# Gathering the base inverse's diagonal blocks once, and another order of the second group of pieces, in a hybrid encoder layer

## The chip, the cores and the metric

The kernel runs on one core of a Trainium2 chip. The metric is the device time of one execution in microseconds (us); lower is better. Engines are named as in the profile: PE (matrix products), PEld (its weight loads), DVE (vector), ACT (scalar and activation functions), POOL (GpSimd) and SP, whose queue issues all the DMAs of this kernel.

## What is computed

One layer of a bidirectional encoder trunk on x of 1024 tokens by 1024 features, float32:

```python
proj = rms_norm(x) @ w_in                       # columns split into aq, ak, av, dqkv, dgate, dalpha, dbeta
attn_o = window_attention(rope(aq), rope(ak), av, sink)        # 8 heads, 2 kv heads, +-128 tokens
dn_o = gated_deltanet(dqkv, dgate, dalpha, dbeta, ...)         # 4 heads, both directions, chunked delta rule
x = x + rms_norm(concat(attn_o, dn_o) @ w_out)
x = x + rms_norm(cross_attention(rms_norm(x), rms_norm(mem)))  # 256 memory tokens
x = x + rms_norm(swiglu(rms_norm(x)))
```

In the delta rule each chunk needs the solution of a triangular system: `tmat = strict_lower(kb k^T * decay) + I`, solved for `v * beta` and `kb * exp(g)`. The kernel forms an inverse of that matrix per chunk of 128 tokens, head and direction. The gate of the delta rule is `o * silu(dgate)`.

## The kernel before

The large products take each float32 operand as a high and a low part (`split`: ACT makes the high part, DVE or POOL the low one), three PE products for one. Weights come in through `load_w` (DMA, then `split`) with a raised priority.

The first third of the kernel is a list of small pieces, named by a letter and a number, and written in three lists by hand: `ORDER_1`, `ORDER_2` and `ORDER_3`. `issue` calls them in that order. The calls only write instructions down. A planner with a simulated clock (`schedule_with_timeline_sim=True`) then makes one fixed queue for each engine: of the instructions that it holds ready, the one written first goes first, and later pieces fill in where earlier ones wait. On the chip each queue runs strictly in that order.

- `D` (`delta_proj`): projections for q, k, v of one delta head, and their convolutions (`conv`: DVE, ACT with SiLU).
- `P` (`prep`): for one head, two halves of four chunks each (`part(b)`). It transposes and normalises k and q, forms the decay `E` (ACT, Exp), stores `kv` to `d_kv`, forms `U` (stored to `d_u`) and `pc`, and multiplies `pc` by an upper and a lower mask on POOL into `pm`, stored to `d_pz` (L482, L483).
- `B` (`base_inverse(g)`): for two heads, both directions. It gathers the 32x32 diagonal blocks of `d_u` into `V` (64 partitions for each direction, both with the same blocks), scales them into `A` (L501, L503), zeroes one triangle on POOL (L504), and inverts all of them by 30 pairs of DVE instructions, each of which needs the one before (L510, L512). The results go to `d_inv` (L519).
- `L` (`levels(h)`): for one head, joins the 32x32 inverses to 64 and to 128 by short chains of products (PE), copies (ACT, DVE, POOL) and transposes, and stores `Z` to `d_pz` (L594). It fetches from `d_inv` (L530).
- `A`, `V`, `G` (`attn_proj`, `value_proj`, `gate_proj`): projections for attention queries (A0 to A3) and keys (A4), attention values, and gates (G0 to G3). Each is 48 PE products of 512 columns (L260). A's results are read from PSUM by DVE (L709, L710); G's by ACT with SiLU (L736), and stored to `d_gate`.
- `W` (`next_windows`): starts two attention windows and finishes the ones started before. Windows use Exp on ACT (L642, L646) and short PE products (L633, L656, L661). Windows 0 to 7 need A4, V, A0 and A1.
- `s`, `K`, `V`, `M` in `ORDER_3`: steps of the scan over the chunks (it reads `d_kv`, `d_pz` and, from its fifth step, `d_gate`), the memory's keys and values, the memory's norm.

The tiles of `prep` (pool `t2`) are followed in SBUF by those of the windows (`tw`) and levels (`tl`). In `base_inverse` the tile `V` has one buffer, as has `vv` in `next_values`.

Of the kernel before, what the change touches and what calls it, by code (L numbers as in the profile page):

```python
# [10 lines left out]
F32 = mybir.dt.float32  # L11
# [3 lines left out]
ALU = mybir.AluOpType  # L15
# [4 lines left out]
P = 128  # L20
# [9 lines left out]
ML = 256  # L30
# [3 lines left out]


ORDER_1 = "D0 P0 D1 P1 D2 P2 D3 P3 B0 B1".split()
ORDER_2 = "G0 G1 G2 G3 L0 L1 V A4 A0 A1 W L2 L3 W W A2 A3 W".split()
ORDER_3 = ("M " + "s01 W K " * 5 + "s01 K " * 3 + "s01 V V").split()


# [35 lines left out]
def tile_hybrid_block(  # L76
# [6 lines left out]
    nc = tc.nc  # L83
# [332 lines left out]
    def together(gens):  # L416

        gens = list(gens)
        while gens:
            gens = [g for g in gens if next(g, g) is not g]  # L420

    def prep(h, kc, qc, vc):

        g, hh = h // 2, h % 2
        def part(b):
            c4 = slice(4 * b, 4 * b + 4)

            def turned(src):
                p_ = small()
                for j in range(4):  # L430
                    o = (4 * b + j) * P
                    nc.tensor.transpose(p_[:, j * P:(j + 1) * P], src[:, o:o + P], ident)
                return p_.rearrange("p (c n) -> p c n", c=4)


            pa = small()
            n = 0
            for d, (mi, ml) in enumerate((("mUi", mL_r), ("mLi", mU_r))):
                for part in (ghi, glo):
                    gm = t2.tile([P, 4, P], F32R, tag="gm", name="gm")  # L440
                    nc.gpsimd.tensor_tensor(gm, bc(part[:, d, h, c4], 2, (P, 4, P)), bc(cm[mi], 1, (P, 4, P)), ALU.mult)
                    nc.tensor.matmul(pa, ml, gm.rearrange("p c n -> p (c n)"), start=(n == 0), stop=(n == 3))
                    n += 1
            E = t2.tile([P, 4, P], F32, tag="E", name="E")
            nc.scalar.activation(E, pa.rearrange("p (c n) -> p c n", c=4), AF.Exp)

            kv = t2.tile([P, 4, 4, P], F32, tag="kv", name="kv")
            for src, i, n, e in ((kc, 0, 1.0, EPS), (qc, 3, float(P), P * EPS)):
                yield
                pk = turned(src)  # L450
                ss = t2.tile([P, 4], F32, tag="ss4", name="ss4", bufs=4)
                for j in range(4):
                    jk = t2.tile([P, P], F32, tag="jk", name="jk")
                    nc.scalar.activation(jk, pk[:, j, :], AF.Square, accum_out=ss[:, j:j + 1])
                rs = t2.tile([P, 4], F32, tag="rs4", name="rs4", bufs=4)
                rstd_of(rs, ss, n, e)
                nc.vector.tensor_tensor(kv[:, :, i, :], pk, bc(rs, 2, (P, 4, P)), ALU.mult)
            yield
            nc.scalar.copy(kv[:, :, 1, :], turned(vc))
            for i, o in ((0, 2), (3, 3)):  # L460
                yield
                p_ = small()
                for j in range(4):
                    nc.tensor.transpose(p_[:, j * P:(j + 1) * P], kv[:, j, i, :], ident)
                nc.scalar.copy(kv[:, :, o, :], p_.rearrange("p (c n) -> p c n", c=4))
            nc.sync.dma_start(d_kv[g][c4, :, hh].rearrange("c p s n -> p c s n"), kv)

            for i in (2, 3):
                yield
                p_ = small().rearrange("p (c n) -> p c n", c=4)  # L470
                for j in range(4):
                    nc.tensor.matmul(p_[:, j, :], kv[:, j, 2, :], kv[:, j, i, :], start=True, stop=True)
                if i == 2:
                    U = t2.tile([P, 4, P], F32, tag="U", name="U")
                    nc.vector.tensor_tensor(U, p_, E, ALU.mult)
                    nc.sync.dma_start(d_u[g][hh, c4].rearrange("c p n -> p c n"), U)
                else:
                    pc = t2.tile([P, 4, P], F32, tag="pc", name="pc")
                    nc.vector.tensor_tensor(pc, p_, E, ALU.mult)
                    for d, mi in enumerate(("mUi", "mLi")):  # L480
                        pm = t2.tile([P, 4, P], F32, tag="pm", name="pm")
                        nc.gpsimd.tensor_tensor(pm, pc, bc(cm[mi], 1, (P, 4, P)), ALU.mult)  # L482
                        nc.sync.dma_start(d_pz[g][d][c4, :, hh, 0].rearrange("c p n -> p c n"), pm)  # L483

        together([part(b) for b in range(2)])

    def base_inverse(g):

        V = tb.tile([P, 32, 32], F32, tag="V", name="V", bufs=1)
        for q in range(4):
            r = slice(32 * q, 32 * q + 32)
            for d in range(2):
                nc.sync.dma_start(V[64 * d + q:64 * d + 64:4], d_u[g].rearrange("h c p n -> (h c) p n")[:, r, r])
        bB = tb.tile([P, 32], F32, tag="bB", name="bB", bufs=1)
        bv = d_beta.rearrange("(d g h c) (b s) -> d g (h c b) s", d=2, g=2, h=2, b=4)
        for d in range(2):
            nc.sync.dma_start(bB[64 * d:64 * d + 64], bv[d, g])
        A = tb.tile([P, 32, 32], F32, tag="A", name="A", bufs=1)  # L500
        nc.vector.scalar_tensor_tensor(A[0:64], V[0:64].rearrange("p r s -> p s r"), -1.0,  # L501
                                       bc(bB[0:64], 1, (64, 32, 32)), ALU.mult, ALU.mult)
        nc.vector.scalar_tensor_tensor(A[64:128], V[64:128], -1.0, bc(bB[64:128], 1, (64, 32, 32)), ALU.mult, ALU.mult)  # L503
        nc.gpsimd.affine_select(out=A, in_=A, compare_op=ALU.is_gt, fill=0.0, base=0,  # L504
                                pattern=[[1, 32], [-1, 32]], channel_multiplier=0)
        tmp = tb.tile([P, 256], F32, tag="tmpb", name="tmpb", bufs=1)
        for j in range(1, 31):
            n = 31 - j
            tv = tmp[:, 0:n * j].rearrange("p (r s) -> p r s", r=n)
            nc.vector.tensor_tensor(tv, A[:, j + 1:, j:j + 1].to_broadcast([P, n, j]),  # L510
                                    A[:, j:j + 1, 0:j].to_broadcast([P, n, j]), ALU.mult)
            nc.vector.tensor_tensor(A[:, j + 1:, 0:j], A[:, j + 1:, 0:j], tv, ALU.add)  # L512
        nc.gpsimd.memset(A.rearrange("p r s -> p (r s)")[:, 0:1024:33], 1.0)
        nc.vector.tensor_tensor(V.rearrange("p r s -> p s r"), A, bc(bB, 2, (P, 32, 32)), ALU.mult)
        nc.gpsimd.tensor_tensor(A, A, bc(bB, 2, (P, 32, 32)), ALU.mult)

        for i in range(2):
            for d in range(2):
                nc.sync.dma_start(d_inv[g][i][d].rearrange("h c b r s -> (h c b) r s"),  # L519
                                  (A if i == d else V)[64 * d:64 * d + 64])  # L520
# [362 lines left out]
    def next_keys():  # L883

        ct = kv_done[0]
        kv_done[0] += 1
        whi, wlo = load_w(w_ckv[:, ct * P:(ct + 1) * P], KT, P, nc.gpsimd)
        pp = pc.tile([P, 512], F32, tag="pc", name="pck")[:, 0:ML]
        for k in range(KT):
            for i, (w, a) in enumerate(((whi, 0), (whi, 1), (wlo, 0))):  # L890
                nc.tensor.matmul(pp, w[:, k, :], mT[a][:, k, :], start=(k == 0 and i == 0), stop=(k == KT - 1 and i == 2))
        cv = mk.tile([P, ML], F32, tag="cv", name="cv", bufs=2)
        nc.scalar.copy(cv, pp)
        nc.sync.dma_start(d_mk[ct * P:(ct + 1) * P, :], cv)

    def next_values():

        ch = kv_done[1]
        kv_done[1] += 1
        pp = [pc.tile([P, 512], F32, tag="pc", name="pcv") for _ in range(2)]  # L900
        for kp in range(4):
            whi, wlo = load_w(w_ckv[kp * 256:(kp + 1) * 256, D + ch * 512:D + (ch + 1) * 512], 2, 512)
            for t in range(2):
                for kk in range(2):
                    k = 2 * kp + kk
                    for i, (w, a) in enumerate(((whi, 0), (whi, 1), (wlo, 0))):
                        nc.tensor.matmul(pp[t], mT[a][:, k, t * P:(t + 1) * P], w[:, kk, :], start=(k == 0 and i == 0),
                                         stop=(k == KT - 1 and i == 2))
        for t in range(2):
            vv = mk.tile([P, 512], F32, tag="vv", name="vv", bufs=1)  # L910
            nc.scalar.copy(vv, pp[t])
            nc.sync.dma_start(d_mv[t, :, ch * 512:(ch + 1) * 512], vv)

# [579 lines left out]
```

## Time and profile before

| | |
|---|---|
| three runs, us | 1604.94, 1600.72, 1600.30 (median 1600.72) |
| profiled execution, us | 1601.45 |
| its span from the first to the last instruction, us | 1599.7 |
| mean granted PE clock | 0.983 |
| PE / DVE / ACT / POOL busy | 95% / 65% / 48% / 33% |
| bytes moved by DMA | 247.29 MB, mean 155 GB/s |

Busy shares count an instruction from its start to its end; PE's products overlap, so PE's share says how seldom it stood still, not how near it was to its peak. "PEclk" is the clock granted to PE, 1.00 or 10 tenths being full speed. In a timeline row, the times are the start and the duration in us, and a bracket holds the idle time of the engine just before it and what ended it.

### The profile page before, as it was taken

How to read it: one execution, taken by the hardware profiler on the slowest of the kernel's cores; microseconds unless marked ns; L12 is line 12 of the kernel's file. 1: busy time of each engine (PE TensorE's matmuls, PEld its weight loads, DVE VectorE, ACT ScalarE, POOL GpSimd, SP SyncE). 2: the span in 40 equal slices, each digit the busy share in tenths (PEclk: the TensorE clock that was granted, in tenths of full speed). 3: DMA queues.
4: the chain of work that ended last, by engine and by line, in shares of the span. 5: the costliest groups of instructions: out<-in, count | busy, mean ns of one | idle time of the engine just before them, and what ended most of it. 6: DMA issues, size and time to landing. Idle time of an engine off the chain costs nothing. (4 is left out here: it accounts for less than half of the span.)

```text
span 1599.7 us, 21414 instructions
## 1 busy us (share of the span) xinstructions
PE 1523.6 (95%) x7558; PEld 1274.7 (80%) x7558; DVE 1034.0 (65%) x1596; ACT 766.2 (48%) x1561; POOL 522.8 (33%) x479
## 2 busy tenths in 40 slices
PE   6999889988899989999999999999999999999998
PEld 5877778877799967788888777778888888888786
DVE  6846886967677765454345549778765555587575
ACT  6566543326957785564334566223322323344532
POOL 2367653234335610243301140335433433100021
PEclk9999999998999999999999999999999999999999
DMA  6134258474999675354222254444333333763344
GB/s 205 41 109 124 59 159 239 129 192 122 296 324 277 193 266 191 145 185 152 73 69 80 90 185 139 150 157 152 100 120 118 104 99 99 272 222 108 110 169 160
DMA packets 265400, 247.29 MB, mean 155 GB/s; under 512 B 43960, under 2 KB 200525, under 8 KB 265293
## 3 DMA queue, kind: packets, MB, share of 16 engines
q1 hardware_dynamic: 265293, 245.93, 48.7%
q8 instruction: 59, 0.97, 0.3%
q14 instruction: 48, 0.39, 0.1%
HBM read 175.86 MB, written 67.40 MB: 152 GB/s over the span
## 5 line engine op out<-in xcount | busy, mean ns | idle before, releaser
L102 ACT CAST whi<-wraw 128x1024 fp32r<-128x1024 f32 x108 | 113.3, 1050 | 147.7 <-PE pA L1166 34.5
L103 POOL TENSOR_TENSOR wlo<-wraw,whi 128x1024 fp32r<-128x1024 f32 x48 | 118.4, 2467 | 165.2 <-ACT whi L102 150.8
L260 PE MATMUL pg<-hhi,whi 128*128 128x512 f32 x352 | 141.5, 403 | 0.0
L260 PE MATMUL pg<-hlo,whi 128*128 128x512 f32 x352 | 140.8, 401 | 0.0
L260 PE MATMUL pg<-hhi,wlo 128*128 128x512 f32 x352 | 140.8, 400 | 0.0
L103 DVE TENSOR_TENSOR wlo<-wraw,whi 128x1024 fp32r<-128x1024 f32 x60 | 75.5, 1260 | 86.0 <-ACT whi L102 76.5
L991 PE MATMUL pmg<-whi,b 128*128 128x512 f32 x384 | 120.0, 400 | 2.6 <-ACT whi L102 2.2
L1166 PE MATMUL pA<-s,whi 128*128 128x512 f32 x352 | 109.7, 393 | 1.4 <-ACT m L1183 1.4
L285 DVE SCALAR_TENSOR_TENSOR acc<-cp,cols,acc 128x1024 f32<-128x1024 f32 x48 | 77.8, 1622 | 34.8 <-ACT acc L283 34.1
L991 PEld LDWEIGHTS pmg<-whi,b 128*128 128x128 f32 x384 | 72.3, 191 | 18.2 <-ACT whi L102 2.7
L1243 POOL TENSOR_TENSOR act<-act,up 128x512 f32<-128x512 f32 x33 | 48.2, 1460 | 103.9 <-DVE up L1242 46.1
L260 PEld LDWEIGHTS pg<-hhi,wlo 128*128 128x128 f32 x352 | 67.5, 192 | 13.3
L260 PEld LDWEIGHTS pg<-hhi,whi 128*128 128x128 f32 x352 | 67.6, 192 | 13.2 <-ACT hhi L102 0.3
L260 PEld LDWEIGHTS pg<-hlo,whi 128*128 128x128 f32 x352 | 67.4, 191 | 13.1
L1354 PE MATMUL pdX<-dhl,whi 128*128 128x512 f32 x264 | 76.1, 391 | 1.5 <-DVE zv L1409 0.8
L1166 PEld LDWEIGHTS pA<-s,whi 128*128 128x128 f32 x352 | 65.3, 188 | 15.2 <-ACT m L1183 2.0
L1384 POOL TENSOR_SCALAR frs<-sq 128x1 f32<-128x1 f32 x8 | 11.9, 1497 | 195.8 <-ACT jk L1373 194.9
L1215 POOL TENSOR_TENSOR sr<-wraw 128x512 f32<-128x512 f32 x22 | 29.0, 1318 | 134.1 <-DMA wraw<-in_w_gate_up_dram 120.9
L991 PE MATMUL pmg<-wlo,b 128*128 128x512 f32 x192 | 71.5, 392 | 0.0
L1166 PE MATMUL pA<-s,wlo 128*128 128x512 f32 x176 | 68.8, 392 | 1.6 <-DVE wlo L103 1.6
L102 ACT CAST whi<-araw 128x1024 fp32r<-128x1024 f32 (+1 forms) x36 | 35.4, 982 | 71.3 <-PE pdX L1354 27.6
L103 DVE TENSOR_TENSOR wlo<-araw,whi 128x1024 fp32r<-128x1024 f32 (+1 forms) x36 | 40.8, 1133 | 39.6 <-ACT whi L102 39.4
(411 smaller groups left out, 4272.5 us busy)
## 6 DMA issues: line engine op xcount, KB each, us to landing
wraw<-in_w_gate_up_dram SPq DMA_DIRECT2D x52, 512.0 KB, 4.1
kv<-d_kv SPq DMA_DIRECT2D x32, 512.0 KB, 6.9
wraw<-in_w_in_dram SPq DMA_DIRECT2D x22, 512.0 KB, 4.0
b<-in_w_down_dram SPq DMA_DIRECT2D x20, 512.0 KB, 5.9
araw<-d_as SPq DMA_DIRECT2D x20, 512.0 KB, 3.8
d_kv<-kv SPq DMA_DIRECT2D x8, 1024.0 KB, 6.3
pz<-d_pz SPq DMA_DIRECT2D x32, 256.0 KB, 6.6
wraw<-in_w_ckv_dram SPq DMA_DIRECT2D x16, 512.0 KB, 6.4
```

Of the source, the lines that this page charges most:

```text
L102: nc.scalar.copy(hi, src)
L103: (eng or nc.vector).tensor_tensor(lo, src, f32(hi), ALU.subtract)
L260: nc.tensor.matmul(p_, w[:, k, :], ah[a][:, k, :], start=(k == 0 and i == 0), stop=(k == nk - 1 and i == 2))
L285: nc.vector.scalar_tensor_tensor(acc, cp[:, t:t + S], taps[t], acc, ALU.mult, ALU.add)
L991: nc.tensor.matmul(pp[t], act[a][:, k, tt], w_[:, kk, :], start=(k == 0 and i == 0), stop=(k == KT - 1 and i == 2))
L1166: nc.tensor.matmul(out_, w[a][:, k, :], xx[b_][:, k, :], start=(start and k == 0 and i == 0), stop=(k == HK - 1 and i == 2), skip_group_ch ...
L1215: nc.gpsimd.tensor_tensor(s[0], b_[:, 0:HK], b_[:, HK:], ALU.add)
L1243: nc.gpsimd.tensor_tensor(o_, o_, up, ALU.mult)
L1354: nc.tensor.matmul(banks[t], a[:, k - k0, tt], w, start=(first and k == 0 and i == 0), stop=(k == NB - 1 and i == 2), skip_group_check=not ...
L1384: nc.gpsimd.tensor_scalar(rs, sq[:, 1, t:t + 1], sq[:, 0, t:t + 1], D * EPS, ALU.add, ALU.add)
```

## The change

`base_inverse` gathers `V` once, into partitions 0 to 63, with four DMAs in place of eight; both halves of `A` are computed from it, with the second direction's beta in a tile of its own, `b1`, with one small load more. The last head's four stores of `pm` are kept back (`unsaved`) and written behind the last `V` load of the second `base_inverse` (`issue_after`); `pm` has three buffers in place of two. `ORDER_2` is written in another order: the four gate projections stand behind L2, L3 and three W. `vv` and `cv` share one tag of two buffers in `next_keys` and `next_values`, in the same number of bytes as before.

```diff
--- before.py
+++ after.py
@@ -34,7 +34,7 @@
 
 
 ORDER_1 = "D0 P0 D1 P1 D2 P2 D3 P3 B0 B1".split()
-ORDER_2 = "G0 G1 G2 G3 L0 L1 V A4 A0 A1 W L2 L3 W W A2 A3 W".split()
+ORDER_2 = "L0 L1 A4 V A0 A1 L2 L3 W W W G0 G1 G2 G3 W A2 A3".split()
 ORDER_3 = ("M " + "s01 W K " * 5 + "s01 K " * 3 + "s01 V V").split()
 
 
@@ -419,6 +419,16 @@
         while gens:
             gens = [g for g in gens if next(g, g) is not g]
 
+    unsaved = []
+
+    def save(after=None):
+
+        while unsaved:
+            with ExitStack() as order_:
+                if after:
+                    order_.enter_context(tc.issue_after(after.ins))
+                nc.sync.dma_start(*unsaved.pop(0))
+
     def prep(h, kc, qc, vc):
 
         g, hh = h // 2, h % 2
@@ -478,9 +488,11 @@
                     pc = t2.tile([P, 4, P], F32, tag="pc", name="pc")
                     nc.vector.tensor_tensor(pc, p_, E, ALU.mult)
                     for d, mi in enumerate(("mUi", "mLi")):
-                        pm = t2.tile([P, 4, P], F32, tag="pm", name="pm")
+                        pm = t2.tile([P, 4, P], F32, tag="pm", name="pm", bufs=3)
                         nc.gpsimd.tensor_tensor(pm, pc, bc(cm[mi], 1, (P, 4, P)), ALU.mult)
-                        nc.sync.dma_start(d_pz[g][d][c4, :, hh, 0].rearrange("c p n -> p c n"), pm)
+                        unsaved.append((d_pz[g][d][c4, :, hh, 0].rearrange("c p n -> p c n"), pm))
+            if h < 3:
+                save()
 
         together([part(b) for b in range(2)])
 
@@ -491,16 +503,19 @@
         V = tb.tile([P, 32, 32], F32, tag="V", name="V", bufs=1)
         for q in range(4):
             r = slice(32 * q, 32 * q + 32)
-            for d in range(2):
-                nc.sync.dma_start(V[64 * d + q:64 * d + 64:4], d_u[g].rearrange("h c p n -> (h c) p n")[:, r, r])
+            load = nc.sync.dma_start(V[q:64:4], d_u[g].rearrange("h c p n -> (h c) p n")[:, r, r])
+        if g:
+            save(load)
         bB = tb.tile([P, 32], F32, tag="bB", name="bB", bufs=1)
+        b1 = tb.tile([64, 32], F32, tag="b1", name="b1", bufs=1)
         bv = d_beta.rearrange("(d g h c) (b s) -> d g (h c b) s", d=2, g=2, h=2, b=4)
         for d in range(2):
             nc.sync.dma_start(bB[64 * d:64 * d + 64], bv[d, g])
+        nc.sync.dma_start(b1, bv[1, g])
         A = tb.tile([P, 32, 32], F32, tag="A", name="A", bufs=1)
         nc.vector.scalar_tensor_tensor(A[0:64], V[0:64].rearrange("p r s -> p s r"), -1.0,
                                        bc(bB[0:64], 1, (64, 32, 32)), ALU.mult, ALU.mult)
-        nc.vector.scalar_tensor_tensor(A[64:128], V[64:128], -1.0, bc(bB[64:128], 1, (64, 32, 32)), ALU.mult, ALU.mult)
+        nc.vector.scalar_tensor_tensor(A[64:128], V[0:64], -1.0, bc(b1, 1, (64, 32, 32)), ALU.mult, ALU.mult)
         nc.gpsimd.affine_select(out=A, in_=A, compare_op=ALU.is_gt, fill=0.0, base=0,
                                 pattern=[[1, 32], [-1, 32]], channel_multiplier=0)
         tmp = tb.tile([P, 256], F32, tag="tmpb", name="tmpb", bufs=1)
@@ -889,7 +904,7 @@
         for k in range(KT):
             for i, (w, a) in enumerate(((whi, 0), (whi, 1), (wlo, 0))):
                 nc.tensor.matmul(pp, w[:, k, :], mT[a][:, k, :], start=(k == 0 and i == 0), stop=(k == KT - 1 and i == 2))
-        cv = mk.tile([P, ML], F32, tag="cv", name="cv", bufs=2)
+        cv = mk.tile([P, 512], F32, tag="cv", name="cv", bufs=2)[:, 0:ML]
         nc.scalar.copy(cv, pp)
         nc.sync.dma_start(d_mk[ct * P:(ct + 1) * P, :], cv)
 
@@ -907,7 +922,7 @@
                         nc.tensor.matmul(pp[t], mT[a][:, k, t * P:(t + 1) * P], w[:, kk, :], start=(k == 0 and i == 0),
                                          stop=(k == KT - 1 and i == 2))
         for t in range(2):
-            vv = mk.tile([P, 512], F32, tag="vv", name="vv", bufs=1)
+            vv = mk.tile([P, 512], F32, tag="cv", name="vv", bufs=2)
             nc.scalar.copy(vv, pp[t])
             nc.sync.dma_start(d_mv[t, :, ch * 512:(ch + 1) * 512], vv)
```

## Prediction

> **What bounds the kernel now.** I read the page first, then windows by stage, then the rows around the two places that the change touches. The page:
>
> ```profile
> PE 1523.6 (95%) x7558; PEld 1274.7 (80%) x7558; DVE 1034.0 (65%) x1596; ACT 766.2 (48%) x1561; POOL 522.8 (33%) x479
> ...
> PEclk9999999998999999999999999999999999999999
> ```
>
> PE bounds the kernel: it stands still for 5% of the span. Time can be won where PE waits, or runs at a lower clock, and nowhere else. PEclk, the granted clock in 40 slices of 40 us, has its only 8 in the tenth slice, at 360 to 400. The windows of that stage (us, busy time of PE, PEld, DVE, ACT, POOL, then PE's granted clock):
>
> ```profile
> 207.00:252.00 45.00, 40.35 (x206) 34.01 (x205) 37.14 (x50) 25.64 (x63) 27.08 (x24) 0.96 0.63 173
> 252.00:274.00 22.00, 22.00 (x102) 18.29 (x101) 12.04 (x12) 5.09 (x8) 7.35 (x6) 1.00 0.91 249
> 274.00:330.00 56.00, 53.77 (x291) 45.54 (x291) 50.52 (x107) 15.65 (x39) 14.50 (x13) 0.97 0.51 142
> 330.00:375.00 45.00, 41.80 (x225) 35.70 (x224) 27.78 (x61) 19.47 (x52) 18.27 (x15) 0.96 0.68 170
> 375.00:425.00 50.00, 40.09 (x211) 32.87 (x211) 34.49 (x78) 36.81 (x100) 21.91 (x25) 0.80 0.62 204
> 425.00:570.00 145.00, 138.67 (x1065) 130.64 (x1064) 109.98 (x294) 106.15 (x298) 74.74 (x79) 1.00 0.86 261
> ```
>
> The same for the large products of the projections alone (L260):
>
> ```profile
> 330.00:375.00 45.00, 30.89 (x121) 0.96 0.68 170
> 375.00:425.00 50.00, 0.71 (x2) 0.80 0.62 204
> ```
>
> From 252 to 274 PE never stops: gate projections fill it while DVE and SP work on the second base inverse. From 375 to 425 there is a hole. PE is idle for 50 − 40.09 = 9.9 us, and its busy 40.09 us run at 0.80 of the clock, which loses another 0.20 × 40.09 = 8.0 us. The large products show why: 30.89 us of them in the 45 us before, 0.71 us in the hole. The last projection (A3) is used up at 375; what is left are L3's short products and the windows', and each waits for ACT or DVE. One gap in it, on PE:
>
> ```profile
> 390.54 1.12 PE L656 MATMUL ptw<-ident,sc 128*128 128x128 f32 x4 [2.80 <-DVE m L635]
> ```
>
> The scan that follows cannot start before L3's last result has been stored:
>
> ```profile
> 322.83 1.44 SPq L519 DMA_DIRECT2D d_inv<-A  x2
> 329.63 0.59 SPq L530 DMA_DIRECT2D cz<-d_inv  x1
> ...
> 405.09 0.36 SPq L594 DMA_DIRECT2D d_pz<-Z  x1
> 414.29 1.19 PE L763 MATMUL psc<-kv,pz 128*128 128x128 f32 x4 [0.36 <-DMA pz<-d_pz]
> ```
>
> So a chain runs from the second base inverse (stored by 324.3) through L2 and L3 (fetched from 329.63, stored at 405.09) to the scan (414.29). Behind it, from 425 to 570, PE is busy 138.67 of 145 us at full clock, and it stays so to the end. What is won or lost by 425 therefore reaches the end undiminished.
>
> **The gather of V.** Here are SP's queue and then DVE, around the second base inverse:
>
> ```profile
> 261.37 2.62 SPq L495 DMA_DIRECT2D V<-d_u  x4
> 264.03 0.62 SPq L483 DMA_DIRECT2D d_pz<-pm  x1
> 264.69 0.54 SPq L495 DMA_DIRECT2D V<-d_u  x1
> 265.76 0.36 SPq L483 DMA_DIRECT2D d_pz<-pm  x1
> 266.17 1.91 SPq L495 DMA_DIRECT2D V<-d_u  x3
> ...
> 269.69 2.07 DVE L501 SCALAR_TENSOR_TENSOR A<-V,bB 64x1024 f32<-64x1024 f32 x1 [5.10 <-DMA V<-d_u]
> 271.79 1.22 DVE L503 SCALAR_TENSOR_TENSOR A<-V,bB 64x1024 f32<-64x1024 f32 x1
> 274.38 0.21 DVE L510 TENSOR_TENSOR tmpb<-A 128x30 f32<-128x30 f32 x1 [1.37 <-POOL A L504]
> ```
>
> Eight loads and two `pm` stores take SP from 261.37 to 268.08; DVE idles 5.10 us for the last of them. Four loads take 2.62 us and end at 263.99, so `V` arrives 4.1 us sooner. The new reading of `V`'s lower half into `A`'s upper half is on the same path: I price it like L503, 1.22 us, no change; the bound is L501's 2.07 us, 0.9 us more. `b1` is one small load, issued long before it is needed, as `bB` is. For the first two heads the same four loads go, but DVE is full there (37.14 of 45 us) with convolutions, and L0 waits for PE until 272; I count nothing.
>
> The kept-back stores cost POOL a wait. The fourth `pm` needs the first one's buffer, which comes free when a store has landed that now stands behind the loads.
>
> ```profile
> 262.21 3.52 POOL L482 TENSOR_TENSOR pm<-pc,C 128x512 f32<-128x512 f32 x2 [4.34 <-DMA d_pz<-pm]
> 273.08 1.26 POOL L504 TENSOR_SCALAR_AFFINE_SELECT A<-A 128x1024 f32<-128x1024 f32 x1 [7.35 <-DVE A L503]
> L483 SPq DMA_DIRECT2D d_pz<-pm x16: 359/360/1074, 112.8 to 265.8; - x16
> DMA to landing us min/median/max: 2.3/2.3/4.4
> ```
>
> Already POOL waits 4.34 us there for such a store. After the change the first store is issued at about 264.0 and lands at 266.3 (2.3 us later); the fourth product takes 1.76 us, to 268.1; L504, queued behind it, is wanted when `A` is written, at 265.6 + 2.07 + 1.22 = 268.9. It just fits. With a landing of 4.4 us it would be 1.3 us late. Nobody reads these stores before the scan. So the base inverse starts 4.1 us sooner (1.9 to 4.1), and its chain of DVE instructions keeps its length. I take 3 us of it on the path, since DVE and SP, which it shares, are not emptied elsewhere.
>
> **The order.** PE's work is the same; only its place changes. The gates are 192 products of 512 columns. A row of the chain of waits has the pace at which such products follow each other at full clock:
>
> ```profile
> 1058.69 2.72 PE pB L1166 x12
> ```
>
> At 0.227 us each, the gates are 43.5 us of PE work that needs nothing but weights and leaves nothing waiting but `d_gate`, which the scan reads only from its fifth step. Before, it fills 207 to 273. After, A4, V, A0 and A1 (equally 192 products) fill that stretch, the windows have their queries some 40 us sooner, and the gates are filler for later. By L2's start the amount of PE time gone by is the same, so every window begun before L2 leaves its PE time in large products for afterwards. I take two windows, about 5 us each (29 products, by rows as above and in the hole; an estimate). So some 10 us of filler reach the hole, and two windows' short products leave it. Ten us of filler against 9.9 us of idle time cannot hit every gap; I take half, 5 us. As the gaps become shorter the clock falls less: half of 8.0, 4 us. With the 3 us that makes 12 us. At the upper end, all losses from 330 to 425 go: 3.2 + 9.9 us idle and 1.7 + 8.0 us of clock are 22.8 us, with 4.1 us for the gather 26.9. At the lower end, nothing.
>
> What the order adds, first on DVE: each early A4, A0 and A1 puts four readings of PSUM, of about 0.69 us, ahead of or among the base inverse's instructions:
>
> ```profile
> 299.88 0.69 DVE L709 TENSOR_TENSOR sn<-pg,sinT 128x512 f32<-128x512 f32 x1
> ```
>
> They stood among them before, too, as this row does, and the windows' DVE work takes their place there; I count 0, up to 4 × 0.69, about +3 us. Then ACT, whose tables are changed between SiLU and Exp:
>
> ```profile
> 235.02 1.28 ACT L445 ACT_TABLE_LOAD   x1
> ...
> 236.93 1.28 ACT L736 ACT_TABLE_LOAD   x1
> 238.22 0.60 ACT L736 ACTIVATE gt<-pg 128x512 f32<-128x512 f32 x1
> ```
>
> The gates and their loads in all, and the windows' loads:
>
> ```profile
> L736 ACT ACTIVATE gt<-pg x8: 590/597/598, 218.0 to 273.2; 128x512 f32<-128x512 f32 x8
> L736 ACT ACT_TABLE_LOAD  x1: 1283/1283/1283, 236.9 to 236.9; - x1
> ```
>
> ```profile
> L642 ACT ACT_TABLE_LOAD  x1: 1283/1283/1283, 365.2 to 365.2; - x1
> ```
>
> Now the eight gate instructions stand next to other SiLUs and cost one load; all windows together cost one. Among windows each gate instruction can cost two. The planner shows no sign of grouping: at 235.02 and 236.93 the tables change twice in 2 us. I expect about ten more loads of 1.283 us, 13 us of ACT; ACT has room from 330 to 375 (19.47 of 45 us) and less later, so a quarter, 3 us, delays somebody (0 to all of 16 × 1.283 = 20.5). The Trainium skill ("ScalarE: Activation LUTs", What ACT_TABLE_LOAD costs, and Rules for kernel authors) speaks against the change here: group functions by table set, and reckon 2.66 us a switch, 1283 ns and a drain. The trace agrees on 1283 ns and shows no drain: the next instruction starts at 238.22, 0.01 us after the load. By the page's price the quarter would be 6.6 us instead of 3.
>
> `vv` with two buffers: no copy into it waited for a buffer in the trace. I count nothing.
>
> The sum: −3 − 9 + 3 = −9 us. The profiled execution took 1601.45 us, 0.73 above the median of 1600.72; from the median, 1591.7.
>
> **The rivals.** *The hole is closed altogether* (12%): the gates and A2, A3 last until the scan starts. For it: the scan is also full, so windows moved ahead cost nothing later. Against: ACT is busy 36.81 of 50 us in the hole and works for L3 in order. −4 − 17 is 1580 (1574 to 1584).
>
> *The hole stays* (20%): the planner fills with gates whenever anything waits, they are gone by 350, and L3 ends as lonely as now; only the gather is left, less its small costs. 1598, within 0.3% (4.8 us), which is about what a measurement of this kernel can tell from no change.
>
> *ACT takes the hole's place* (24%), slower: gate SiLUs fall between the Exps of six windows just while L2 and L3 need ACT for their copies. Fourteen loads and eight gate instructions are 14 × 1.283 + 8 × 0.597 = 22.7 us on ACT; two thirds of it on the chain is +15, less 3 for the gather and 4 for filler is +8: 1609. It decides once more than half of these 22.7 us lies ahead of something on the chain. For it: ACT's queue is strict, and from 425 on ACT is busy 106.15 of 145 us; against it: 25 us of ACT are free from 330 to 375.
>
> **How the numbers follow.** Forecast 44%: 1592, from 1584 to 1597. The range leaves out about one in ten on either side: 1581, inside the closed hole, to 1609, the middle of the slower rival. Faster by over 0.3% (below 1595.9): nearly all of the forecast and the closed hole, 0.54; same 0.21; slower 0.25.
>
> **What would show it.** Right: `V`'s last load of the second base inverse near 264 and L501 near 265.6; large products in the last 50 us before the scan's first product; granted clock there above 0.9; that product at about 404. Wrong: the gates' PE work over before L2's fetch; more than twelve ACT table loads among windows, with level copies waiting behind them; or the base inverse's DVE chain longer by more than it starts sooner.

## The result: slower, and the profile after

| | before | after |
|---|---|---|
| median, us | 1600.68 (1596.45 to 1604.94, 10 runs) | 1607.10 (1604.33 to 1613.96, 10 runs) |
| ratio to before | | 1.0052, 95% interval 1.0039 to 1.0066 |
| profiled execution, us | 1601.45 | 1607.53 |
| its span, us | 1599.7 | 1605.8 |

The change costs 6.4 us by the medians, some 8 us by the ratio, where 9 us were forecast as gain. The page after, busy time and granted clock:

```profile
PE 1517.6 (95%) x7558; PEld 1269.3 (79%) x7558; DVE 1043.3 (65%) x1596; ACT 773.5 (48%) x1567; POOL 522.7 (33%) x479
...
PEclk9999999899999999999999999999999999999999
```

The 8 has moved from the tenth slice (360 to 400) to the eighth (280 to 320). The windows of the kernel after, columns as in the prediction:

```profile
207.00:252.00 45.00, 39.88 (x199) 32.93 (x198) 33.45 (x47) 21.68 (x58) 26.38 (x24) 0.92 0.54 145
252.00:274.00 22.00, 22.00 (x125) 19.06 (x124) 19.25 (x24) 6.61 (x17) 9.32 (x8) 1.00 0.95 250
274.00:330.00 56.00, 48.43 (x238) 40.92 (x237) 53.05 (x117) 23.99 (x56) 22.94 (x21) 0.88 0.53 147
330.00:375.00 45.00, 39.76 (x225) 33.34 (x224) 29.92 (x60) 33.23 (x74) 13.99 (x12) 1.00 0.63 159
375.00:425.00 50.00, 46.37 (x262) 39.74 (x261) 34.16 (x74) 34.83 (x89) 22.48 (x23) 0.97 0.54 152
425.00:570.00 145.00, 134.96 (x1056) 128.21 (x1056) 108.45 (x291) 99.86 (x281) 69.70 (x77) 1.00 0.90 274
570.00:680.00 110.00, 96.19 (x400) 76.22 (x399) 53.66 (x55) 56.60 (x91) 11.93 (x18) 0.94 0.60 209
```

The last stretch is the memory's keys and values behind the scan. It was not shown of before; there it is

```profile
570.00:680.00 110.00, 102.10 (x446) 82.89 (x445) 57.30 (x70) 65.10 (x110) 11.88 (x20) 0.95 0.60 207
```

Call PE's idle time plus (1 − clock) × busy time the loss of a stretch. It can be laid side by side:

| stretch | loss before | after | difference |
|---|---|---|---|
| 207 to 252 | 4.6 + 1.6 | 5.1 + 3.2 | +2.1 |
| 274 to 330 | 2.2 + 1.6 | 7.6 + 5.8 | +9.6 |
| 330 to 375 | 3.2 + 1.7 | 5.2 + 0.0 | +0.3 |
| 375 to 425 (the hole) | 9.9 + 8.0 | 3.6 + 1.4 | −12.9 |
| 425 to 570 | 6.3 + 0.0 | 10.0 + 0.0 | +3.7 |
| 570 to 680 | 7.9 + 5.1 | 13.8 + 5.8 | +6.6 |

That is +9.4; with 0.9 more ahead of 207 and 2.1 less from 680 to 1590 it is about +8, for a span longer by 6.1. The clock is printed to 0.01, so each clock term is good to half a us or so. The hole closed as forecast; the loss came back ahead of it, while the base inverse runs, and behind it, where the prediction said that nothing would. Up to 425 the account comes out even: 0.9 + 2.1 + 9.6 + 0.3 − 12.9 = 0.0. The kernel is slower by what it loses behind.

The large products alone (L260) show the hole filled, 23.65 us where there were 0.71:

```profile
330.00:375.00 45.00, 21.56 (x90) 16.31 (x89) 1.00 0.63 159
375.00:425.00 50.00, 23.65 (x92) 16.54 (x92) 0.97 0.54 152
```

The base inverse in the kernel after, from the timeline (SP's queue, DVE, POOL):

```profile
264.30 3.15 SPq L506 DMA_DIRECT2D V<-d_u  x4
...
269.71 1.99 DVE L516 SCALAR_TENSOR_TENSOR A<-V,bB 64x1024 f32<-64x1024 f32 x1 [0.48 <-DMA V<-d_u]
270.53 2.29 POOL L492 TENSOR_TENSOR pm<-pc,C 128x512 f32<-128x512 f32 x1 [9.09 <-DMA d_pz<-pm]
271.72 2.18 DVE L518 SCALAR_TENSOR_TENSOR A<-V,b 64x1024 f32<-64x1024 f32 x1
...
275.78 1.28 DVE L525 TENSOR_TENSOR tmpb<-A 128x30 f32<-128x30 f32 x1 [0.52 <-POOL A L519]
...
328.19 2.09 DVE L529 TENSOR_TENSOR V<-A,bB 128x1024 f32<-128x1024 f32 x1
...
334.38 0.36 SPq L545 DMA_DIRECT2D cz<-d_inv  x1
...
428.25 0.68 PE L778 MATMUL psc<-kv,pz 128*128 128x128 f32 x4 [0.77 <-DMA pz<-d_pz]
```

Nothing is won by the gather: the four loads start later than the eight did, `A` starts at 269.71 (269.69 before), its second half takes 2.18 us (1.22), the chain begins 1.4 us later and is 8 us longer, and L2 fetches at 334.38 (329.63). Behind the scan, two gaps on PE that before has not:

```profile
601.28 2.07 PE L922 MATMUL pcv<-whi,mT 128*128 128x512 f32 x4 [5.85 <-ACT whi L102]
615.89 2.88 PE L1006 MATMUL pmg<-whi,s 128*128 128x512 f32 x8 [3.47 <-ACT whi L102]
```

ACT itself waited there for the weights' DMA, in the waits of 560 to 640 of the kernel after:

```profile
ACT whi L102 <- DMA wraw<-in_w_ckv_dram: 11.3, 4, 5.7
```

In the kernel before the same wait is 1.3 us, once: windows were still running beside those weights until 614. In the kernel after the last one ends at 595.

### The profile page after: what moved, and what is told of

The parts are those of the page before. It is cut to its first block, busy times and chain, and to the rows that moved or that the text cites. A ratio compares the mean times of both kernels' runs of the same rounds, so it can differ in the third digit from the quotient of the medians.

```text
span 1605.8 us, 21413 instructions
## 1 busy us (share of the span) xinstructions
PE 1517.6 (95%) x7558; PEld 1269.3 (79%) x7558; DVE 1043.3 (65%) x1596; ACT 773.5 (48%) x1567; POOL 522.7 (33%) x479
## 5 line engine op out<-in xcount | busy, mean ns | idle before, releaser
L260 PE MATMUL pg<-hlo,whi 128*128 128x512 f32 x352 | 141.5, 402 | 0.0
L260 PE MATMUL pg<-hhi,whi 128*128 128x512 f32 x352 | 141.4, 403 | 0.0
L260 PE MATMUL pg<-hhi,wlo 128*128 128x512 f32 x352 | 141.2, 402 | 0.0
L260 PEld LDWEIGHTS pg<-hhi,whi 128*128 128x128 f32 x352 | 68.0, 194 | 13.6 <-ACT hhi L102 0.3
L260 PEld LDWEIGHTS pg<-hlo,whi 128*128 128x128 f32 x352 | 68.1, 193 | 13.2
L260 PEld LDWEIGHTS pg<-hhi,wlo 128*128 128x128 f32 x352 | 67.9, 193 | 13.1
```

The source lines that it names most:

```text
L260: nc.tensor.matmul(p_, w[:, k, :], ah[a][:, k, :], start=(k == 0 and i == 0), stop=(k == nk - 1 and i == 2))
```

## The experiments

All ratios are to the kernel before, run beside each kernel on the same chip. "Moved" counts the PE products, of 7066, that stand elsewhere in the written queue than in the kernel before. The number hangs on which products are taken as alike, so only its size should be read.

### The parts of the change, and the activation tables

e1 is the gather with the kept-back stores and the third `pm` buffer, in the old order; e2 the new `ORDER_2` alone; e3 the shared tag of `cv` and `vv` alone. e4 is the kernel after with the gates' SiLU left out (Identity in its place):

```diff
-            nc.scalar.activation(gt, pp[hf], AF.Silu)
+            nc.scalar.activation(gt, pp[hf], AF.Identity)
```

> Only the gather of V, the kept-back pm stores and the third pm buffer; the order of the second list and vv as before. Theory P (place): the new order costs what the change costs, so this one is within 3 us of before (about 1600), with the hole from 375 to 425 still there (PE busy near 40 of 50 us). Rival T (activation tables): the same, since the gates stay together. Rival G (gather): the gather with POOL's wait for the pm stores makes the base inverse late, so this one alone is 5 to 8 us slower than before.

> Only the new order of the second list, on the kernel before. P: slower than before by 5 to 10 us, hole from 375 to 425 closed (PE busy above 45 of 50 us), more idle time from 207 to 330 and from 570 to 680. T: the same size, with eight table loads among the windows. G: within 3 us of before.

> Only the shared tag of two buffers for cv and vv, on the kernel before. P, T and G: within 2 us of before. If the idle time from 570 to 680 comes from this edit, it is 3 to 7 us slower and shows PE waiting there for weights of the memory's values.

> The changed kernel with the gates' SiLU left out (Identity in its place, so the gate is not applied as the reference has it): the queues of PE, DVE and SP are those of the changed kernel, and ACT lacks only its table changes around the gates, 7 or 8 of 1.283 us. T: 5 to 10 us faster than the changed kernel, so about as fast as before. P and G: within 2 us of the changed kernel, 1605 to 1609.

| | median, us | ratio, 95% interval |
|---|---|---|
| e1 | 1615.01 | 1.0101 (1.0076 to 1.0127) |
| e2 | 1610.45 | 1.0073 (1.0046 to 1.0099) |
| e3 | 1599.74 | 1.0004 (0.9985 to 1.0024) |
| e4 | 1607.92 | 1.0043 (1.0023 to 1.0064) |

The tables fall as a cause. The kernel after has these loads among gates and windows (groups by line):

```profile
L751 ACT ACT_TABLE_LOAD x4 | 5.1, 1283 | 0.1
L657 ACT ACT_TABLE_LOAD x3 | 3.8, 1283 | 0.1
...
L661 ACT ACT_TABLE_LOAD x1 | 1.3, 1283 | 0.0
```

e4 has none of the eight, and its time lies in the interval of the kernel after, so the 5 to 10 us that were expected of the tables are not there; a cost of some 3 us would not show between these two intervals. The shared tag does nothing in the old order. e1, expected within 3 us of before or 5 to 8 slower, is 14.6 slower. It and e2 cost more apart (1.0% and 0.7%) than together (0.5%), so no theory that adds up the parts holds.

### Windows as filler behind the scan

e5 moves three W of the kernel after behind the gates, A2 and A3. e16 is the same order without the gather; e2 is its partner with the change's order. e8 keeps the old order but for G3 and one W.

```diff
-ORDER_2 = "L0 L1 A4 V A0 A1 L2 L3 W W W G0 G1 G2 G3 W A2 A3".split()
+ORDER_2 = "L0 L1 A4 V A0 A1 L2 L3 W G0 G1 G2 G3 A2 A3 W W W".split()
```

> The kernel after with one thing moved: in the second list only one W stands ahead of the gates, the other three behind A2 and A3. In the written queues 45 of the windows' products stand ahead of the scan (98 in the kernel after) and 51 behind its last product (9 after, 36 before); 58 large products stand behind the last level's transposes (76 after). Theory W (the windows were spent as filler ahead of the scan and are missing where the memory's values wait for their weights): the loss between 570 and 680 falls from 19.6 to 13 us or less, the hole at 375 to 425 stays closed (loss of 7 us or less), the total comes 4 to 7 us below the kernel after, at 1600 to 1603. Theory C (the base inverse's longer chain and the later scan cost the time, wherever the windows are): the total stays at 1605 to 1609, and what the tail gains is lost between 375 and 570.

> The kernel before with the second list alone in the order L0 L1 A4 V A0 A1 L2 L3 W G0 G1 G2 G3 A2 A3 W W W, which with the gather, the kept-back stores and the third buffer gave 1600.3. 53 of the windows' products stand behind the scan's last. Theory W (late windows mend the new order): the loss at 570 to 680 is 13 us or less where the change's order without the gather lost 21.8, and the total is 4 us or more below that kernel's 1610.5. If the gather is worth something in this order, this kernel is slower than 1600.3 by 3 us or more; if it is worth nothing, both lie within 3 us.

> The kernel before with another order of the second list alone: G0 G1 G2 L0 L1 V A4 A0 A1 W L2 L3 W G3 A2 A3 W W, so three gates stay where they were, G3 stands behind L3 and one W, and the last two W behind A3. 40 large products stand behind the level transposes of the last head's first half (none before), 41 of the windows' products behind the scan (36 before). Theory W with the hole's reading from the first profile: the hole's loss falls from 17.9 to 10 us or less, the stages at 207 to 330 lose no more than 3 us over before, since gates fill them as before, the tail loses 14 us or less, and the total is 1592 to 1597. Theory R: the total is anywhere between 1595 and 1612, and the hole's gain shows up as a loss elsewhere.

| | median, us | ratio, 95% interval | loss 274–330, 375–425, 570–680 |
|---|---|---|---|
| after | 1607.10 | 1.0052 (1.0039 to 1.0066) | 13.4, 5.0, 19.6 |
| e5 | 1600.28 | 1.0020 (1.0004 to 1.0035) | 13.7, 9.5, 9.4 |
| e2 | 1610.45 | 1.0073 (1.0046 to 1.0099) | 17.4, 5.5, 21.8 |
| e16 | 1603.91 | 1.0028 (1.0015 to 1.0042) | 14.3, 6.6, 9.5 |
| e8 | 1603.01 | 1.0021 (1.0004 to 1.0039) | 8.7, 9.5, 10.2 |

The windows of 570 to 680 in e5, then in e2 and in e16:

```profile
570.00:680.00 110.00, 103.70 (x466) 84.24 (x465) 62.45 (x81) 73.48 (x133) 15.89 (x23) 0.97 0.62 209
```

```profile
570.00:680.00 110.00, 94.78 (x424) 77.68 (x423) 58.27 (x71) 64.77 (x112) 13.50 (x23) 0.93 0.60 203
```

```profile
570.00:680.00 110.00, 102.52 (x462) 82.58 (x461) 62.25 (x83) 71.27 (x128) 15.95 (x24) 0.98 0.62 206
```

Twice, moving the W alone takes 10 to 12 us of loss out of the tail and some 5 to 7 us off the time (0.32% and 0.45%, by the ratios). The expected 13 us or less was met; e5's hole, expected at 7 us or less, has 9.5, and e8 missed its 1592 to 1597. So the place of three W is most of what the change cost, and the tail is where most of it shows. It is not the whole: e5, e16 and e8 lose less than before in the tail and about half as much or less in the hole, and are still not faster than before; from 274 to 330 they lose 9 to 14 us where before lost 3.8. e5 and e16 are apart by 3.6 us in their medians, but the kernel before, run beside each, is apart by 2.1 (1597.09 and 1599.20), and the intervals of the ratios overlap: in this order the gather is worth little, if anything.

Why the later windows help is not shown as closely. They may cover the wait for the memory's weights; but in e5 ACT also waits less for these weights (2.7 us, not 11.3), and the memory's values start at 562.8, not 578.1. And the second pair is not the windows alone. e2 has 29 of the windows' products behind the scan, nearly as many as before (36). Its longest gap there is another, at the copy of `vv`, which has one buffer in e2 and stands in ACT's queue behind three casts that wait for their DMA:

```profile
619.72 1.22 PE L991 MATMUL pmg<-whi,s 128*128 128x512 f32 x2 [8.21 <-ACT vv L911]
```

### The gather and the stores, apart and with nothing in them

e6 has only the gather (stores in place, two buffers), e7 only the kept-back stores with the third buffer, e13 only the third buffer. e14 loads `V` eight times but computes `A`'s second half as the change does; e15 is e6 with its four loads cut in halves.

```diff
-                        pm = t2.tile([P, 4, P], F32, tag="pm", name="pm")
+                        pm = t2.tile([P, 4, P], F32, tag="pm", name="pm", bufs=3)
```

(e13, the whole edit.)

> The kernel before with V gathered once (four loads, b1, both halves of A from partitions 0 to 63), the stores of pm where they were and two buffers of pm. The gather with the kept-back stores cost 14.6 us. Theory A (the new half of A beside POOL costs): 1602 to 1605, since that half took 0.95 us more and its loads came sooner. Theory K (the kept-back stores and the third buffer cost): 1598 to 1602. Theory R (neither step costs in its own place; the planner, given other instructions, writes other queues for the stages behind, and these are worse by chance): the total is away from 1600.4 by 3 us or more in either direction, with the base inverse's chain no longer than before and the loss in stages behind 330.

> The kernel before with the last head's stores of pm kept back behind the last V load and three buffers of pm, V gathered by eight loads as before. Theory K: 1608 or more, with the wait in POOL's or SP's queue near 265. Theory A: 1598 to 1602. Theory R: away from 1600.4 by 3 us or more in either direction with the loss behind 330; and what the gather alone and the stores alone cost does not add up to the 14.6 us of both together within 4 us.

> The kernel before with three buffers of pm in place of two and nothing else: the same instructions, and a wait that can only go. In the written queues 710 of PE's 7066 products stand elsewhere than before, from the 490th on. Theory R (the planner's other queues for the stages behind are the cost, whatever makes it write them): 1606 or more, away from the kernel before by 5 us or more, with the loss between 274 and 680. Theory K' (what is added or kept back costs by itself): 1598 to 1602, since nothing is added.

> The kernel before with eight loads of V as before, but the second half of A computed from partitions 0 to 63 of V with b1, as in the change. The written queues are nearly those of before: 56 of PE's 7066 products stand elsewhere. Theory R: 1598 to 1603, as before, though the new half of A takes about 1 us longer than the old. Theory A (the new half and its load are what costs): 1606 or more.

> The gather alone (1611.4), with each of its four loads cut into two of half the size, so that eight loads stand in the queue as before and as many bytes move as with four. 363 of PE's products stand elsewhere than in the kernel before (563 with four loads). Theory R: somewhere between 1600 and 1612, wherever the queues lead, and not by what the loads cost: V is in place no later than in the kernel before. Theory A: 1608 to 1612 again.

| | moved | median, us | ratio, 95% interval |
|---|---|---|---|
| e14 half of A | 56 | 1600.85 | 1.0002 (0.9986 to 1.0019) |
| e15 half loads | 363 | 1608.55 | 1.0067 (1.0045 to 1.0089) |
| e7 stores | 550 | 1612.84 | 1.0099 (1.0078 to 1.0119) |
| e6 gather | 563 | 1611.43 | 1.0081 (1.0065 to 1.0097) |
| e1 all three | 697 | 1615.01 | 1.0101 (1.0076 to 1.0127) |
| e13 third buffer | 710 | 1607.34 | 1.0056 (1.0036 to 1.0075) |

e13 is the plain case: the same instructions, with waits that can only go, and 0.56% slower in other queues. Gather and stores cost 0.81% and 0.99% apart and 1.01% together. e14 does the disputed arithmetic in nearly the old queues and costs nothing; e15 does not decide, since both theories allowed its time. So the new half of `A` is not what e1 pays for, and other queues can cost 0.56% by themselves. That they are what the gather and the stores pay for fits, but is not shown: neither was run in the old queues. Nor does the count alone price an edit, for the queues of e5, e8, e11 and e16 differ from those of before by more than e13's do, and they cost 0.1 to 0.3%. Which of the moved instructions does it is not settled. e13's profiled execution took 1617.92 us, 10.6 above its median; of the loss that it has over before, 11 us are at 274 to 425, 9 of them in the clock:

```profile
274.00:330.00 56.00, 51.88 (x261) 43.56 (x259) 48.28 (x106) 16.42 (x41) 14.18 (x12) 0.88 0.48 134
330.00:375.00 45.00, 37.44 (x181) 30.73 (x181) 25.97 (x43) 10.84 (x29) 16.12 (x12) 0.92 0.63 161
375.00:425.00 50.00, 44.18 (x210) 38.41 (x210) 29.36 (x75) 34.28 (x91) 20.61 (x22) 0.75 0.43 123
```

### A suspect that was wrong: the queries' cast on ACT

In e1, e6 and e7 ACT stands long at the first window's cast of its queries, with the levels' copies queued behind. From e1's timeline (8.91 us in before):

```profile
357.87 0.62 ACT L639 CAST qs<-qr 128x512 fp32r<-128x512 f32 x1 [14.33 <-DMA qr<-d_q]
```

e9 (on e1), e10 (on before), e11 (on e5) and e12 (on e8) write the first windows' casts behind the levels' copies:

```diff
+            cp = nc.scalar.copy(mov6[0:64], Z[1][0:64, :, 0:64])
+            if h == 2:
+                behind[0] = cp
...
+        with ExitStack() as order_:
+            if n < 2 and g == 0:
+                order_.enter_context(tc.issue_after(behind[0].ins))
+            nc.scalar.copy(qs, qr)
```

In e9, e10 and e12 the first W stands behind L3 as well.

> The gather with the kept-back stores (1613 to 1615 us, as the gather alone and the stores alone), with the first W behind L2 and L3 in the second list and the casts qs of the first two windows placed behind the copies mov of the levels of head 2 on ACT. In those three kernels ACT stands 12.6 to 14.3 us at the first of these casts, until 355.9 to 357.9, waiting for the queries' load (8.9 us until 352.9 in the kernel before), with the levels' copies bs, m and z queued behind it. Theory Q (that cast, in front of the levels' copies, is what costs): the level's first bs copies come before 350, the last Z store comes at 400 or sooner, the loss between 330 and 425 falls from 28.6 to 20 us or less, and the total falls by 6 us or more, to 1608 or less. Theory R' (the loss is spread over the stage and hangs on the whole interleaving): within 4 us of 1614, or the gain in 330 to 425 is lost again behind.

> The same edit on the kernel before, without the gather and the kept-back stores. Theory Q: the cast's 8.9 us in the kernel before are too a wait in front of the levels; the scan starts sooner than 414, and the total falls by 2 to 6 us below the kernel before, so 1592 to 1596 at a before of 1598; and it lies within 3 us of the gather's kernel with the same edit, since the gather itself costs nothing. Theory R': the total is within 3 us of the kernel before or above it.

> The kernel after with one W ahead of the gates (1600.3 us) and the same placement of the casts qs. Theory Q: the ACT wait for the queries' load (8.7 us there) no longer holds the levels, and the total falls by 2 to 5 us to 1595 to 1598, below the kernel before by up to 2 us. Theory R': 1598 to 1606.

> The kernel before with three gates first, G3 behind L3 and two W, all W behind L3, and the same placement of the casts qs; without the cast's placement and with the first W ahead of L2 it was 1603.0. Theory Q: with the hole filled (9.5 us lost against 17.9) and the casts out of the way of the levels, 1592 to 1598, the fastest of all kernels here. Theory R': 1598 to 1608.

| | median, us | ratio, 95% interval |
|---|---|---|
| e9 | 1615.54 | 1.0099 (1.0071 to 1.0127) |
| e10 | 1613.27 | 1.0082 (1.0052 to 1.0113) |
| e11 | 1602.36 | 1.0011 (0.9991 to 1.0031) |
| e12 | 1608.86 | 1.0046 (1.0024 to 1.0068) |

The theory falls: e9 gains nothing on e1, and e10 loses 12 us on before, with the casts and the first W moved together, though its scan starts 5 us sooner (414.29 before):

```profile
409.08 1.06 PE L770 MATMUL psc<-kv,pz 128*128 128x128 f32 x4
```

So a sooner scan alone brings no time. But a late one goes with a slow kernel in these runs. By the profiled executions the scan's first product comes at 409.9 to 414.3 in before, e3, e5, e8, e11, e14, e16 and e18, which all lie within 0.28% of before. It comes at 419.0 to 432.4 in the kernel after, e1, e2, e4, e6, e7, e13, e15 and e17, which cost 0.43 to 1.01%. Only e9, e10 and e12, where the first W stands behind L3 as well, are slow with 409.1 to 416.9. Moving the three W also brought this product from 428.25 to 411.51 (after to e5) and from 432.36 to 410.41 (e2 to e16). So the windows' place in the tail and the start of the scan were not separated, and whether a late scan costs time or only shows what was lost ahead of it is open.

### POOL beside the base inverse's chain

The chain's 60 instructions are two groups of 30 in the view by line. In the kernel before, then in the kernel after:

```profile
L512 DVE TENSOR_TENSOR A<-A,tmpb 128x30 f32<-128x30 f32 (+14 forms) x30 | 12.8, 426 | 0.9
L510 DVE TENSOR_TENSOR tmpb<-A 128x30 f32<-128x30 f32 (+14 forms) x30 | 11.2, 373 | 2.1 <-POOL A L504 1.4
```

```profile
L525 DVE TENSOR_TENSOR tmpb<-A 128x30 f32<-128x30 f32 (+14 forms) x30 | 16.3, 543 | 1.2 <-POOL A L519 0.5
L527 DVE TENSOR_TENSOR A<-A,tmpb 128x30 f32<-128x30 f32 (+14 forms) x30 | 14.8, 494 | 0.7
```

The same instructions take 24.0 us and 31.1 us: 7.1 of the 8 us by which the chain is longer. POOL is busy 14.50 us from 274 to 330 before and 22.94 after, with rotations (L730) and windows' splits that the new order brings there. It is the order and not the gather: in e2 and e16, which have the order alone, the 60 instructions take 28.9 us, and in e1 and e6, which have the gather in the old order, 24.7. e17 adds eight POOL multiplications to the kernel before, e18 eight fills of 1024 columns in their place; PE's, ACT's and DVE's queues stay the same, instruction for instruction.

```diff
+        if g:
+            dm = V.rearrange("p r s -> p (r s)")[:, 0:512]
+            for _ in range(8):
+                nc.gpsimd.tensor_tensor(dm, sinT[:, 0:512], cosT[:, 0:512], ALU.mult)
```

> The kernel before with eight multiplications of 512 columns added on POOL behind the triangle's zeroing of the second base inverse (two operands in SBUF, about 1.27 us each, into V, which nobody needs just then; their result is not used). The written queues of PE, ACT and DVE are those of the kernel before, instruction for instruction; POOL has eight more. Theory L (a DVE instruction with two operands in SBUF stands still while a POOL instruction that reads SBUF runs): the base inverse's DVE instructions beside them take 1 us or more each in place of 0.2 to 0.4; of the chain's 60 instructions (24.0 us together in the kernel before, 31.1 in the kernel after) the sum rises by 5 us or more, and the chain ends 5 us or more later than 318.7. Theory N (the kernel after's DVE instructions are slow for another reason, such as a fuller DVE queue): the sum stays within 1 us of 24.0. The total: if the chain's end is on the path, 4 us or more above the kernel before; if PE finds other work, within 3 us.

> The same place with eight instructions on POOL that only write (fills of 1024 columns of V, which nobody needs just then). PE's, ACT's and DVE's written queues are those of the kernel before. If it is POOL's reading that holds DVE: the chain's 60 instructions stay within 1 us of 24.0 in sum, and the total within 3 us of the kernel before. If any work on POOL holds DVE: the sum rises by about as much as these eight take.

The groups and the first rows beside POOL in e17:

```profile
L516 DVE TENSOR_TENSOR A<-A,tmpb 128x30 f32<-128x30 f32 (+14 forms) x30 | 15.0, 499 | 0.9
L514 DVE TENSOR_TENSOR tmpb<-A 128x30 f32<-128x30 f32 (+14 forms) x30 | 14.8, 493 | 2.1 <-POOL A L504 1.4
...
273.80 11.73 POOL L509 TENSOR_TENSOR V<-sinT,cosT 128x512 f32<-128x512 f32 x8
273.86 1.27 DVE L514 TENSOR_TENSOR tmpb<-A 128x30 f32<-128x30 f32 x1 [1.37 <-POOL A L504]
```

And in e18:

```profile
L516 DVE TENSOR_TENSOR A<-A,tmpb 128x30 f32<-128x30 f32 (+14 forms) x30 | 12.8, 426 | 0.9
L514 DVE TENSOR_TENSOR tmpb<-A 128x30 f32<-128x30 f32 (+14 forms) x30 | 11.3, 378 | 2.1 <-POOL A L504 1.4
...
273.35 8.04 POOL L509 MEMSET V<- 128x1024 f32 x8
273.44 0.21 DVE L514 TENSOR_TENSOR tmpb<-A 128x30 f32<-128x30 f32 x1 [1.37 <-POOL A L504]
```

With reading work on POOL the chain's instructions take 29.8 us (+5.8) and it ends at 324.62, 5.9 later; with 8.04 us of fills they take 24.1. An instruction of 0.21 us takes 1.27 when it starts beside a POOL multiplication: it waits for the end of it. The median of e17 is 1609.05 us, ratio 1.0058 (1.0045 to 1.0071), of e18 1601.80, 1.0015 (1.0000 to 1.0030). So in the old order's queues POOL's reading costs the whole some 7 us, with a chain 5.9 us later and the scan's first product at 420.57 (414.32 in e18):

```profile
420.57 1.19 PE L767 MATMUL psc<-kv,pz 128*128 128x128 f32 x4 [0.76 <-DMA pz<-d_pz]
```

e17's profiled execution is its fastest, 1601.04 us, with no more loss in sum than before; it is 8 us under the median of five, and no trace shows where a usual execution loses them. Nor does it follow that the change pays as much: e5's 60 instructions take 29.9 us, nearly those of the kernel after, and its scan starts sooner than before.

## Why the prediction was wrong

**The hole** (right, and undersized). It was there for want of large products, and they closed it: loss from 17.9 to 5.0, −12.9 where −9 was forecast. The clock there rose from 0.80 to 0.97, above the 0.9 that was named as a sign.

**"What is won or lost by 425 therefore reaches the end undiminished"** (wrong, the step that made an even kernel a slower one). It was read off one row, 138.67 of 145 us at full clock, and the prediction's windows end at 570. From 570 to 680 the kernel before already lost 13.0 us. Of the windows' 260 products (their transposes aside) 36 stand in the written queue behind the scan's last product before, and 9 after. The forecast took "two windows, about 5 us each" from elsewhere at no cost; behind 425 the kernel after loses 3.7 and 6.6 us more. e5 has W there again: it loses 4.0 and 10.2 us less behind 425 than the kernel after, 4.5 more in the hole, and is some 5 us faster. That windows cover the memory's weights is the likely reason, not a shown one.

**The gather, −3** (wrong; the chain's start came 1.4 us later). The 4.1 us counted eight loads against four from the same start. But `U` came later, and the loads ran from 264.30 to 267.45, not 261.37 to 263.99; `A` began at 269.71, not 265.6. The new half of `A` cost 2.18 us, just over the bound of 2.07 and not the 1.22 taken. e14 and e7 show why. With POOL idle the same instruction takes 1.22 us (e14); beside POOL's last `pm` the old form of it takes 2.16 (e7):

```profile
270.51 1.22 DVE L505 SCALAR_TENSOR_TENSOR A<-V,b 64x1024 f32<-64x1024 f32 x1
...
270.16 2.16 DVE L517 SCALAR_TENSOR_TENSOR A<-V,bB 64x1024 f32<-64x1024 f32 x1
```

In the kernel after, that `pm` ran beside it from 270.53. It is the wait that "just fits": the product ended at 272.82, with 9.09 us waited, not at 268.1.

**"Its chain of DVE instructions keeps its length"** (wrong by 8 us; from 274 to 330, where it runs, the kernel after loses 9.6 us more, which with the 2.1 of 207 to 252 uses up nearly all that the hole gave). The forecast looked at what else stands in DVE's queue, 0 to +3 us, and not at POOL. The Trainium skill ("SBUF — State Buffer", SBUF: two separate sides) has the rule that was missed: DVE and GpSimd share one port pair under an exclusive lock, and a DVE instruction with two SBUF inputs contends for it only with a GpSimd instruction that reads SBUF. The trace agrees on both halves: e17's multiplications hold DVE for 5.8 us, e18's fills for 0.1.

**ACT's tables, +3** (not seen; too small for e4 to refute). There are eight loads where the forecast had ten more than two. The rival that ended near the measured time, ACT in the hole's place at 1609, has its number by luck: without the loads e4 takes as long, and the hole closed. The Trainium skill ("ScalarE: Activation LUTs", Rules for kernel authors) budgets about 2.7 us for every switch to a different set, and would have priced them higher still. No run here shows such a price.

**The scan's first product at about 404** (wrong, 428.25). L3's results were stored by 406.5, 1 us later than before in place of sooner, since the base inverse was later. After that the first scan load stood in SP's queue behind stores of the last projection's results, which the new order puts at the end:

```profile
423.18 0.34 SPq L731 DMA_DIRECT2D d_q<-rop  x1
...
424.06 0.43 SPq L787 DMA_DIRECT2D pz<-d_pz  x1
```

PE had filler meanwhile.

**`vv`, nothing** (right in the old order: 1.0004). In the new order it was not run alone; the 8.21 us of e2 suggest that it matters there.

**What the prediction did not have at all** is the planner as a source of scatter. It went through the edits one at a time and priced each against the old queues. But five edits around the base inverse that rewrote 363 to 710 of PE's positions cost 0.6 to 1.0% each, one of them with no work in it, and the one that left the queues nearly alone cost nothing. Beside that, terms of 3 us could not decide the sign. What in those queues costs the time stays open, as said above; the late scan that they share is the nearest lead. No variant here is faster than the kernel before; e3, e11 and e14 are level with it.

## What to carry to other kernels

Filler that closes one hole is taken from somewhere: find the stage that loses it, read the windows to the end of the kernel, and price it as lost. Where a planner writes the queues, see whether an edit moves a few positions or hundreds before pricing its parts, and run an edit without work in it (one more buffer) to learn how far the time scatters. Work that POOL reads from SBUF can lengthen a chain on DVE: look at what POOL runs beside it before and after.

## What the runs showed of the hardware that was not expected

A POOL multiplication that reads SBUF holds DVE instructions with two SBUF operands until it ends: 0.21 us became 1.27, 1.22 became 2.18. POOL seems to lose as well: eight multiplications took 11.73 us in e17, 1.47 each, while three rotations of the same size in the kernel after (L730, 275.72 to 285.96) took 1.26 to 1.29. DVE instructions with one operand in PSUM (L561 and L562 of the levels in the kernel before) kept their 0.68 us beside them, and beside eight POOL fills the chain took 24.1 us, as before. Eight activation table loads more or less, 10.3 us of ACT, made no difference that e4's runs can tell from none.
